# A two-layer diffusion trunk on one core: every SBUF pool laid out anew, with the moving operands and the next weights of TensorE at chosen distances modulo 256 bytes

## The chip, the core and the metric

The kernel runs on one core of one Trainium2 chip. The metric is the device time of one execution in microseconds; the time before is the median of three runs.

## The reference, cut to what matters

Two layers work on 512 latent tokens and 256 context tokens of width 1024, all in float32. Layer 0 is neighbourhood attention beside a spatial gating unit, layer 1 is a two-way retention over the latent tokens with a state carried in from the context; behind each comes a gated MLP with a depthwise convolution over the tokens. Every sub-layer stands between two RMS norms, and shift, scale and gate come from a conditioning vector.

```python
h = modulate(rmsnorm(x, norm_g[i, 0]), sh1, sc1)
y = hybrid_na_sgu(...) if i % 2 == 0 else retention_mixer(...)
x = x + g1 * rmsnorm(y, norm_g[i, 1])
h = modulate(rmsnorm(x, norm_g[i, 2]), sh2, sc2)
a = dwconv3(h @ ffn_w_in[i], conv_w, conv_b)        # 1024 -> 2 * 2816
gate, up = split(a)
x = x + g2 * rmsnorm((silu(gate) * up) @ ffn_w_out[i], norm_g[i, 3])
```

Nearly all of the arithmetic is in the products with the weight matrices.

## The kernel before, in words

**Products in three parts.** A float32 operand is split in two float32r tiles: `split` lets ScalarE (ACT) write the rounded value, hi, and VectorE (DVE) the rest, lo. `mm3` then issues three matmuls for every product: hi by hi, hi by lo, lo by hi. Its first argument is the stationary operand (128 columns, loaded by a weight load before each matmul), its second the moving one, of 256, 384 or 512 columns. The weight load of a matmul is issued while the matmul before it still streams. So while one matmul reads its moving operand, the weights of the next are read out of the same SBUF partitions.

**Weight units.** A unit is 128 x 1024 elements of a weight matrix. `raw_unit` loads it by a DMA of the SyncE (SP) queue into a `raw` tile, `unit` splits it into the hi and the lo tile of a slot. There are three slots in the lasting pool `bp` (tags `wh0`, `wl0` to `wh2`, `wl2`) and some more in a pool of the stage (`slot`, `phase`): two in the gating unit, three in the retention, and named rings in the MLPs (the inner function `slot` of `ffn`). In some products the unit is stationary and the activations move (the projections of attention, the queries and keys of the retention, the first products of the MLPs); in others the activations are stationary and the unit moves (gating unit, the retention's values and gates, all output projections).

**The stages in order.** Gating unit (output tiles `ug`, `mx`, `wsg`), attention (`pq`, `pk`, `pv`, for the context `px` and `py`; scores `s`, weighted values `o`, output `wat...`), MLP of layer 0 (`px`, `py`, `pz` of 384 columns, from a two-by-two block scheme with fewer multiplications; output `wf`), retention (values and gates `rn`, keys and queries `rk`, `rq`, context keys `rkc`, scores `rs`, states `stc`, `stl`, results `ro`, `rx`, output `wr`), MLP of layer 1 (`px`, `py`, `pz` of 256 columns, output `wf`). Vector products for shift, scale and gate run beside them as background jobs. Nearly every instruction is recorded under line 69, a helper, so the profile's groups are told apart by their tiles.

**Where tiles lie.** A pool takes its tags in the order of their first use, each with the room of all its buffers, and rounds a tile up to 32 bytes; pools follow one another, and a pool of a stage begins where the pools still open end. So every tile's byte address in its partition can be worked out from the sizes. Three lines of `retention` and three of `ffn` already create tiles early to fix an order. Below, the position of a tile is its address modulo 256, and the distance of a matmul is the position at which the weights of the next matmul begin, minus the position at which its own moving operand begins, modulo 256.

Of the kernel before, what the change touches and what calls it, by code (L numbers as in the profile page):

```python
# [18 lines left out]
KD = 8  # L19
# [14 lines left out]
EARLY = 2  # L34
MLP_PIECES = (
# [41 lines left out]
class Trunk:  # L77
    def __init__(self, ctx, tc, a, out):
        self.ctx, self.tc, self.nc, self.a, self.out = ctx, tc, tc.nc, a, out
        nc = self.nc  # L80
        self.V, self.S, self.T = (Ordered(tc, e) for e in (nc.vector, nc.scalar, nc.tensor))
        self.G = nc.gpsimd
        pool = lambda name, **k: ctx.enter_context(tc.tile_pool(name=name, bufs=1, **k))
        self.cp = pool("cp")
        self.bp = pool("bp")
        self.pp = pool("pp", space=bass.MemoryType.PSUM)
        self.dp = pool("dp", space=bass.MemoryType.DRAM)
        self.flip = 0

# [29 lines left out]
    def slot(self, name):  # L119
        i = self.turn % (3 + self.extra)  # L120
        self.turn += 1
        pool = self.bp if i < 3 else self.xp
        return [pool.tile([P, 1024], F32R, name=f"{name}{x}", tag=f"w{x}{i}", bufs=1) for x in "hl"]

    def phase(self, ctx, name, extra):
        self.xp = ctx.enter_context(self.tc.tile_pool(name=name, bufs=1))
        self.extra = extra
        self.turn = 0
        return self.xp

# [8 lines left out]
    def setup(self):  # L139
# [4 lines left out]
        c4 = self.cp.tile([P, KD, 4], F32R, name="c4", tag="c4")  # L144
        for s in range(2):
            S.activation(c4[:, :, 2 * s], cs[:, 8 * s : 8 * s + 8], AF.Copy)
            V.tensor_tensor(
                out=c4[:, :, 2 * s + 1],
                in0=cs[:, 8 * s : 8 * s + 8],
                in1=c4[:, :, 2 * s].bitcast(F32),  # L150
                op=ALU.subtract,
            )
        self.c4 = c4
        self.ident = self.const("ident", [P, P], a["ident"])
        self.adab = self.const("adab", [P, 16], a["adab_col"])
        self.ng = self.const("ng", [P, 64], a["ng_col"])
# [18 lines left out]
    def ada_first(self, q, pool, native, tag):  # L175
# [5 lines left out]
        for n in range(2):  # L181
# [24 lines left out]
            if not native:  # L206
                mt = self.bp.tile([P, 2, 4], F32, name=f"mt{n}{q}", tag="mt", bufs=2)
                S.copy(mt, pt)
# [31 lines left out]
    def ada_half(self, l, half, streams, gate=None, away=False, fine=False, side=False):  # L240
# [60 lines left out]
        gi = (l * 4 + (0 if m < 2 else 2)) * 8 + h * 4  # L301
# [227 lines left out]
    def block_sums(self, l):  # L529
# [30 lines left out]
        hb = self.bp.tile([P, 6144], F32R, name=f"hs{l}", tag="h1", bufs=1)  # L560
        for i, x in enumerate((2, 4)):
            self.blk["t", x] = hb[:, 8 * n * i : 8 * n * (i + 1)].rearrange("p (x k c) -> p x k c", x=2, k=4)
        self.rest = hb[:, 16 * n :]
# [142 lines left out]
    def sgu(self, y, xn):  # L706
        S, V, T, G, a = self.S, self.V, self.T, self.G, self.a
        toks = (4, 5, 0, 1, 2, 3)
        with ExitStack() as ctx:
            wp = self.phase(ctx, "sguw", 2)  # L710
            bcol = wp.tile([P, 8], F32, name="sgub", tag="sgub")
            self.load(bcol, a["sgu_b"])

            def ug_units(which, js):
                return [
                    self.unit(a["hyb_ug"][(which * 4 + i) * P : (which * 4 + i + 1) * P], f"ug{which}{i}") for i in js
                ]
# [9 lines left out]
            with ExitStack() as c2:  # L727
                fp = c2.enter_context(self.tc.tile_pool(name="firstp", bufs=1))
                self.alloc_h("a")
# [27 lines left out]
            sp = ctx.enter_context(self.tc.tile_pool(name="sgup", bufs=1))  # L757
            u = [sp.tile([P, 6, 256], F32, name=f"un{i}", tag=f"un{i}") for i in range(2)]
# [3 lines left out]
            for t in toks:  # L762
                ug(ps[t], t, w, (6, 7))
                gg = self.t2k(f"gg{t}")
                S.activation(gg, ps[t], AF.Gelu_apprx_tanh)
                bs = sp.tile([P, 6], F32, name=f"bs{t}", tag="bs", bufs=2)
                mv = sp.tile([P, 2], F32, name=f"mv{t}", tag="mv", bufs=2)
# [46 lines left out]
            wo = [self.unit(a["hyb_out"][(4 + f) * P : (5 + f) * P], f"wos{f}") for f in range(4)]  # L814
# [8 lines left out]
    def attention(self, y, final):  # L823
        a = self.a
        with ExitStack() as ctx:
            ap = self.ap = self.phase(ctx, "attp", 0)
            self.mask = ap.tile([P, 3, 256], F32, name="mask", tag="mask")
# [15 lines left out]
            for i in range(n + lag):  # L843
                if i < n:
# [3 lines left out]
                    if step == 0:  # L848
                        pr["at"] = [ap.tile([P, 768], F32R, name=f"at{x}{j}", tag=f"at{x}", bufs=4) for x in range(2)]
                        if j == 3:  # L850
                            A = (
                                [pairs[0]["at"], pairs[1]["at"]],
                                [self.unit(a["hyb_out"][f * P : (f + 1) * P], f"woa{f}") for f in (0, 1)],
                            )
                            fills = self.out_pieces(*A, y, toks[:1], False, None, "ata", "A")
# [220 lines left out]
    def retention(self, y, final):  # L1076
        S, V, T, G, a = self.S, self.V, self.T, self.G, self.a
        KS = float(np.float32(P) ** np.float32(-0.5))
        with ExitStack() as ctx:
            rp = self.phase(ctx, "retp", 3)  # L1080
# [10 lines left out]
            order = [("rv0", 1536), ("rv1", 1536), ("rg", 1024)] + [(f"w{x}{i}", 1024) for i in (3, 4, 5) for x in "hl"]  # L1091
            order += [("e0", ND), ("e1", ND), ("rk0", 512), ("rk1", 512), ("rq0", 512), ("rq1", 512), ("kd0", 1024), ("kd1", 1024)]
            for tag, w in order:
                rp.tile([P, w], F32, name=f"at{tag}", tag=tag, bufs=1)
# [3 lines left out]
                self.unit(a["ret_vg"][(o + h * 2 + i) * P : (o + h * 2 + i + 1) * P], f"rw{n}{h}{i}", dst)  # L1098
# [299 lines left out]
    def ffn(self, l, y, final, gates=None):  # L1398
# [13 lines left out]
        with ExitStack() as ctx:  # L1412
            fp = self.phase(ctx, f"ffnp{l}", 0)
            cw = fp.tile([P, 44, 4], F32, name=f"cw{l}", tag="cw")
            if not first:
                for tag in ("rawu", "wh5", "wl5", "wh6", "wl6", "pre0", "pre1"):
                    fp.tile([P, 1024], F32R if tag[0] == "w" else F32, name=f"at{tag}", tag=tag, bufs=1)
# [5 lines left out]
            if first:  # L1423
                G.memset(pres[0][:, :, 256:258], 0.0)
            else:
                for tag in ("cv", "wh4", "wl4"):
                    fp.tile([P, 1024], F32R if tag[0] == "w" else F32, name=f"at{tag}", tag=tag, bufs=1)
# [7 lines left out]
            def slot(kind, name):  # L1435
# [6 lines left out]
                if h[0] == "w":  # L1442
                    pool = self.bp if i < 3 else fp
                    return [pool.tile([P, 1024], F32R, name=f"{name}{x}", tag=f"w{x}{i}", bufs=1) for x in "hl"]
# [43 lines left out]
            def conv(j, pre):  # L1488
# [16 lines left out]
                else:  # L1505
                    g = [fp.tile([P, W], F32R, name=f"g{l}{i}{j}", tag=f"g{i}", bufs=ng) for i in range(2)]
# [103 lines left out]
            def w_out(f, kind="o"):  # L1610
                u = slot(kind, f"fo{l}{f}")
# [148 lines left out]
    def build(self):  # L1760
# [11 lines left out]
        def ahead(key, src, home):  # L1772

            dst = [self.bp.tile([P, 1024], F32R, name=f"{key}{x}", tag=f"w{x}{home}", bufs=1) for x in "hl"]
# [12 lines left out]
        with ExitStack() as ctx:  # L1787
# [18 lines left out]
            self.early = hook(("rwv00", ("ret_vg", 0), 0), ("rwv01", ("ret_vg", 1), 1))  # L1806
            self.between = lambda: ahead("rwk0", ("ret_qk", 8), 2)
# [74 lines left out]
def layout(i):  # L1882
# [8 lines left out]
    o["ng_col"] = cols(g["norm_g"])  # L1891
# [40 lines left out]
```

## Time and profile before

| what | value |
|---|---|
| median of three runs | 1865.7 us (1861.69 to 1869.01) |
| span of the profiled execution | 1867.9 us |
| TensorE matmuls | 1797.4 us busy, 96% of the span, 10928 instructions |
| TensorE weight loads | 1591.9 us busy, 85% |
| VectorE, ScalarE, GpSimd | 75%, 55%, 17% |
| mean granted clock of TensorE | 0.986 |

The profile gives no time for the profiled execution beside its span; the span stands 2.2 us above the median of the runs, inside their range. Matmuls are pipelined: the duration in a row runs from a matmul's start to its modelled end and is longer than the time until the next one starts. Rows of one tile give the smallest, the median and the largest duration. Two rows of one shape can be compared by their durations, and the true pace comes from the starts of successive groups in the timeline.

### The profile page before, as it was taken

Reading aid. Unit: us, or ns where it says so; the run is one execution under the profiler, and the core shown is the slowest. Engines: PE = TensorE matmul, PEld = TensorE weight load, DVE = VectorE, ACT = ScalarE, POOL = GpSimd, SP = SyncE. Lnnn points to the kernel's source line nnn. Section 1 sums busy time; section 2 is a strip of 40 time slices with the busy share of each in tenths; the row PEclk is TensorE's granted clock in tenths of the full one; section 3 lists DMA queues with packets and bytes.
Section 4 is the critical chain, followed back from the end, with each engine's and each line's share of the span. In section 5 each row is a group of like instructions: output and inputs, shape, how many; then the busy total and the mean of one; then the engine's idle time right before and its main releaser. Section 6 shows DMA issues by size and latency. Waiting matters only on the chain. (4 is left out here: it accounts for less than half of the span.)

```text
span 1867.9 us, 28825 instructions
## 1 busy us (share of the span) xinstructions
PE 1797.4 (96%) x10928; PEld 1591.9 (85%) x10928; DVE 1400.7 (75%) x2359; ACT 1031.0 (55%) x1866; POOL 325.9 (17%) x462
## 2 busy tenths in 40 slices
PE   7999999999999999999898999999999989999997
PEld 4887777689998899998788989988999879889996
DVE  4877775789868778777766676676655699988887
ACT  6533555677555565554564535344344477667763
POOL 1102222031122222221111011011001100222221
PEclk9999999999999999999899999999999989999999
DMA  8345321255677777786622423332321325978772
GB/s 293 113 139 149 108 85 40 69 157 154 170 148 194 167 164 159 156 169 149 243 98 76 156 79 99 116 95 70 113 69 46 102 81 153 224 192 197 172 162 97
DMA packets 84399, 253.47 MB, mean 136 GB/s; under 512 B 11026, under 2 KB 11538, under 8 KB 84260
## 3 DMA queue, kind: packets, MB, share of 16 engines
q1 hardware_dynamic: 55044, 191.29, 32.7%
q0 software_dynamic: 26912, 51.95, 16.4%
q10 hardware_dynamic: 2304, 8.39, 1.1%
q8 instruction: 86, 1.41, 0.3%
q14 instruction: 53, 0.43, 0.1%
HBM read 191.81 MB, written 39.85 MB: 124 GB/s over the span
## 5 line engine op out<-in xcount | busy, mean ns | idle before, releaser
L69 DVE SCALAR_TENSOR_TENSOR acc<-ar,cs,acc 128x512 f32<-128x512 f32 x256 | 185.5, 750 | 32.0 <-DMA ar<-in_adaw 17.4
L69 DVE SCALAR_TENSOR_TENSOR cv<-pre,cw,cv 128x769 f32<-128x769 f32 (+1 forms) x176 | 153.4, 881 | 9.9 <-ACT cv L69 9.2
L1645 POOL DMA_DIRECT2D yf<-yp x64 | 55.1, 861 | 257.0 <-ACT yp L69 235.5
L69 ACT ACTIVATE cv<-pre,cw 128x770 f32<-128x770 f32 (+1 forms) x88 | 81.2, 924 | 20.3 <-DVE pre L69 19.7
L69 ACT COPY yp<-wf 128x512 f32<-128x512 f32 x118 | 67.8, 577 | 23.7 <-PE wf L69 23.4
L69 ACT ACTIVATE pre<-px 128x256 f32<-128x256 f32 (+2 forms) x160 | 54.3, 366 | 48.1 <-PE px L69 47.4
L1645 POOL DMA_DIRECT2D yd<-yp x48 | 43.0, 902 | 132.1 <-ACT yp L69 129.1
L1645 POOL DMA_DIRECT2D yd<-ypg x48 | 41.9, 882 | 132.8 <-ACT ypg L69 124.3
L1265 POOL TENSOR_SCALAR rrr<-rmv 128x2 f32<-128x2 f32 x16 | 3.8, 237 | 274.1 <-DVE rmv L69 274.0
L69 ACT ACTIVATE g<-cv 128x770 fp32r<-128x770 f32 (+1 forms) x44 | 32.4, 736 | 29.1 <-DVE cv L69 29.1
L69 PE MATMUL px<-hs,wd 128*128 128x384 f32 x240 | 46.1, 340 | 0.2 <-DVE pre L69 0.2
L246 POOL MEMSET acc<- 128x512 f32 x32 | 19.3, 606 | 147.7 <-DVE al L69 128.9
L69 PEld LDWEIGHTS px<-hs,wd 128*128 128x128 f32 x240 | 43.0, 191 | 2.2 <-DVE pre L69 0.6
L69 DVE TENSOR_TENSOR pre<-pre,pz 128x256 f32<-128x256 f32 (+1 forms) x60 | 20.8, 372 | 29.9 <-PE pz L69 29.9
L69 DVE TENSOR_TENSOR g<-cv,g 128x770 fp32r<-128x770 f32 (+1 forms) x44 | 36.2, 822 | 8.3 <-ACT g L69 8.2
L69 ACT ACTIVATE pre<-py 128x384 f32<-128x384 f32 (+1 forms) x40 | 17.5, 437 | 43.4 <-PE py L69 23.1
L69 ACT ACTIVATE cv<-cv 128x770 f32<-128x770 f32 (+1 forms) x44 | 32.7, 743 | 14.2 <-DVE cv L69 14.1
L69 DVE TENSOR_TENSOR rv<-rn,rv 128x512 fp32r<-128x512 f32 x24 | 16.5, 687 | 30.2 <-ACT rv L69 30.2
L69 ACT ACTIVATE sc<-sc,sst 128x512 f32<-128x512 f32 x32 | 23.1, 723 | 27.7 <-DVE sc L69 27.7
L69 DVE TENSOR_TENSOR cv<-cv 128x770 f32<-128x770 f32 (+1 forms) x44 | 36.2, 823 | 1.1
L69 ACT COPY ypg<-wf 128x512 f32<-128x512 f32 x54 | 30.9, 577 | 9.7 <-PE wf L69 8.8
L69 ACT ACTIVATE rv<-rn 128x512 fp32r<-128x512 f32 x24 | 14.3, 594 | 38.5 <-PE rn L69 37.6
(2645 smaller groups left out, 6905.8 us busy)
## 6 DMA issues: line engine op xcount, KB each, us to landing
ar<-in_adaw SPq DMA_DIRECT2D x96, 512.0 KB, 3.8
yf<-yp POOLq DMA_DIRECT2D x64, 256.0 KB, 4.7
yd<-yp POOLq DMA_DIRECT2D x54, 256.0 KB, 5.2
yd<-ypg POOLq DMA_DIRECT2D x54, 256.0 KB, 4.9
fin<-xd SPq DMA_DIRECT2D x8, 512.0 KB
xn<-in_x SPq DMA_DIRECT2D x6, 512.0 KB, 4.6
xb<-in_x SPq DMA_DIRECT2D x6, 512.0 KB
xd<-xb ACTq DMA_DIRECT2D x6, 512.0 KB, 3.2
```

Of the source, the lines that this page charges most:

```text
L69: i = f(*args, **kw)
L246: G.memset(t, 0.0)
L1265: G.tensor_scalar(out=rr[:, 0, t2], in0=mv[:, t2, 1], scalar1=1.0, scalar2=EPS, op0=ALU.mult, op1=ALU.add)
L1645: G.dma_start((yd[t] if first else y[t])[:, o], v, accum_op=ALU.add)
```

## The change

**One slot, one tile.** hi and lo of a unit are no longer two tiles of 1024 elements but two parts of one tile (`place`): in the slots of `bp` and of the retention it has 2112 elements, and the unit begins `at` elements into it, 0, `Q1` = 16 or `Q3` = 48 (0, 64 or 192 bytes); the other slots have 2048 elements, and the pool's order sets their position.

**Every pool gets a written order.** A new helper `lay` creates one tile of each tag before all use, with nameless gaps of 16, 24, 40 or 48 elements, in `bp` and in the pools of the gating unit, the attention, the retention and both MLPs. No instruction is issued for these tiles.

**Small moves.** `c4` (the split conditioning vector) and `mt` go to the pool of the first stage, with the four instructions that fill `c4`; `bs` and `mv` of the gating unit go to `bp`; `ng` holds only the 32 of its 64 columns that are read; the second half of `h1` behind the blocks begins 64 bytes later; `g` of the first MLP lies 62 elements into a tile of 832, so that the latent tokens' columns begin at position 0 and the context's at 248.

The positions, worked out from the sizes (w0 to w2 are slots in `bp`):

| matmuls (columns) | stationary / moving | distance before | distance after |
|---|---|---|---|
| `rn` (256) | h / unit | 192 (w0, w1), 128 (w2), 224 (w3 to w5) | 64 |
| `ug` of the second half (256) | h / unit | 192, 128, 96 | 64 |
| `ug` of the first half, `wsg` (512) | h or sT / unit | 192, 128, 96 or 96, 32, 0 | 0 |
| `pq`, `pk` / `pv` (512) | unit / h | 64 / 128 | 0 |
| `px`, `py` of the attention (256) | unit / h | 64 and 128 | 0 |
| `s` (256) | q / k | 0 | 64 |
| `px`, `py`, `pz` of layer 0 (384) | unit / blocks | 0, 64, 128 | 64 (`wd` 0) |
| `px`, `py`, `pz` of layer 1 (256) | unit / blocks | 0 or 64 | 64 |
| `wf` of layer 0 (512) | g / unit | many | 0 (latent), 248 (context) |
| `wf` of layer 1 (512) | g / unit | 0 (w5, w6), 192 (w2) | 0 |
| `rk`, `rq` (512) | unit / h | 64, 128, 32 | 0 |
| `rkc` (256) | unit / h | 64, 128, 32 | 0 |
| `rs` (256) | k / q | 0 | 64 |
| `stc`, `stl`, `ro` (256) | kd, sd / v | 64 | 64 |
| `rx` (512) | q / st | 0 | 0 |
| `wr` (512) | gt / unit | 224 (w0, w1), 160 (w2), 0 (w3 to w5) | 0 |

The diff, cut to its core:

```diff
+SLOT = 2112
+Q1, Q3 = 16, 48
 ...
+        order = [("G0", 1024), ("h0", 6144), ("t2k", 512, 4), ("y0", 1024), ("y1", 1024), ("y2", 1024), ("y3", 1024)]
+        order += [("raw", 1024, 3), ("w0", SLOT), ("w1", SLOT), ("w2", SLOT), ("acc0", 512), ("h1", 6144 + Q1)]
+        order += [("ss", 2, 8), ("rsw", 1, 4), ("rsr", 1, 6), ("bs", 6, 2), ("mv", 2, 2)]
+        self.lay(self.bp, order)
...
-    def unit(self, src, name, dst=None):
+    def unit(self, src, name, dst=None, at=0):
         raw = self.raw_unit(src, name)
-        hi, lo = dst or self.slot(name)
+        hi, lo = dst or self.slot(name, at)
         self.split(hi, lo, raw)
...
+    def place(self, i, name, at=0):
+        pool, wide = (self.bp, SLOT) if i < 3 else (self.xp, self.wide)
+        if wide == 2048:
+            at = 0
+        t = pool.tile([P, wide], F32R, name=name, tag=f"w{i}", bufs=1)
+        return [t[:, at + 1024 * x : at + 1024 * x + 1024] for x in range(2)]
...
+    def lay(self, pool, order):
+        for n, (tag, width, *bufs) in enumerate(order):
+            if tag is None:
+                tag = f"gap{n}"
+            pool.tile([P, width], F32, name=f"at{tag}", tag=tag, bufs=bufs[0] if bufs else 1)
...
-        return [pool.tile([P, 1024], F32R, name=f"{name}{x}", tag=f"w{x}{i}", bufs=1) for x in "hl"]
+        return self.place(i, name, at)
...
+            order = [("dist", ND), ("cos", 512), ("sin", 512), ("dec", 16), ("gng", 16), (None, 24)]
+            order += [("rv0", 1536), ("rv1", 1536), ("rg", 1024), ("w3", SLOT), ("w4", SLOT), ("w5", SLOT)]
+            order += [("e0", ND), ("e1", ND), (None, 16), ("rk0", 512), ("rk1", 512), (None, 48), ("rq0", 512), ("rq1", 512)]
+            order += [("kd0", 1024), ("kd1", 1024), ("kc", 256), ("sd0", 512, 2), ("sd1", 512, 2), (None, 48), ("of", 1024)]
...
+                order = [("rawu", 1024), ("w5", 2048), ("w6", 2048), ("pre0", 1024), ("pre1", 1024), ("blk", 4096), ("cv", 1024)]
+                order += [(None, 16), ("w3", 2048), (None, 48), ("g0", W, 4), ("g1", W, 4), (None, 16), ("w4", 2048)]
+                order += [("cw", 176), ("yp", 2048)]
```

More of the change, by code (lines that the diff above doesn't have):

```diff
@@ L715, in ug_units @@
                 return [
-                    self.unit(a["hyb_ug"][(which * 4 + i) * P : (which * 4 + i + 1) * P], f"ug{which}{i}") for i in js
+                    self.unit(
+                        a["hyb_ug"][(which * 4 + i) * P : (which * 4 + i + 1) * P], f"ug{which}{i}", at=0 if which else Q3
+                    )
+                    for i in js
                 ]
@@ L1442, in slot @@
                 if h[0] == "w":
-                    pool = self.bp if i < 3 else fp
-                    return [pool.tile([P, 1024], F32R, name=f"{name}{x}", tag=f"w{x}{i}", bufs=1) for x in "hl"]
+                    return self.place(i, name, at)
                 pool = self.bp if i < 4 else self.lp
```

89 lines of the change are left out of this document (47 added, 42 removed).

## The prediction

> **What bounds the kernel now.** I read the page first, then the busy times by stage, then the timeline of one place, then the rows of single tiles.
>
> ```profile
> span 1867.9 us, 28825 instructions
> PE 1797.4 (96%) x10928; PEld 1591.9 (85%) x10928; DVE 1400.7 (75%) x2359; ACT 1031.0 (55%) x1866; POOL 325.9 (17%) x462
> PEclk9999999999999999999899999999999989999999
> PE 36%; DVE 5%; ACT 3%; DMA 2%; issue 1%; POOL 1%; DVEq 0%; ACTq 0%; POOLq 0%; SPq 0%
> ```
>
> TensorE is busy for 96% of the span at a granted clock that is full in nearly every slice, and it leads the chain of waits. By stage (first MLP's main loop, seven heads of the retention, second MLP's main loop; columns: stretch, its length, busy time and count of each engine, clock, DMA):
>
> ```profile
> 436.00:930.00 494.00, 478.82 (x2432) 438.70 (x2431) 397.62 (x567) 283.09 (x490) 110.39 (x146) 0.98 0.73 171
> 1030.00:1460.00 430.00, 428.59 (x2993) 393.99 (x2992) 269.42 (x460) 184.42 (x264) 39.98 (x56) 1.00 0.30 93
> 1545.00:1834.00 289.00, 285.88 (x2007) 264.34 (x2006) 255.51 (x400) 201.64 (x357) 57.31 (x68) 1.00 0.72 176
> ```
>
> PE runs for 478.82 of 494, 428.59 of 430 and 285.88 of 289 us; the next engine, DVE, has 20%, 37% and 12% to spare. So the time is the sum of the intervals at which matmuls follow each other, and a nanosecond off each of 10928 is 10.9 us.
>
> **Does that interval depend on where the operands lie?** In the timeline (start, length, engine, tile, count) two groups of the same twelve matmuls, at the same distance of 64, both before and after:
>
> ```profile
> 1208.76 1.52 PE L69 MATMUL ro<-rv,sd 128*128 128x256 f32 x12
> 1210.12 1.08 PE L69 MATMUL rx<-st,rq 128*128 128x512 f32 x4
> ...
> 1214.24 1.58 PE L69 MATMUL ro<-rv,sd 128*128 128x256 f32 x12
> 1215.66 1.55 PE L69 MATMUL rx<-st,rq 128*128 128x512 f32 x6
> ```
>
> From start to start it is (1210.12 - 1208.76) / 12 = 113 ns and (1215.66 - 1214.24) / 12 = 118 ns. So a distance does not fix the interval alone; a stream can run in one of two paces. Durations follow the interval: 113 ns goes with 276 and 118 with 281, 162 or 163 ns more each time, so rows can be compared by their medians. Now equal work in slots at different positions. The output projection of the retention (distance 0 in the first row, 224 in the second) and its context keys (64 and 128):
>
> ```profile
> L69 PE MATMUL wr<-rwo10h,gt x16: 388/389/497, 1097.6 to 1108.9; 128*128 128x512 f32 x16
> L69 PE MATMUL wr<-rwo20h,gt x16: 392/396/495, 1163.4 to 1175.0; 128*128 128x512 f32 x16
> ...
> L69 PE MATMUL rkc<-h0c,rwk1h x8: 276/276/383, 1011.3 to 1014.8; 128*128 128x256 f32 x8
> L69 PE MATMUL rkc<-h0c,rwk2h x8: 279/282/285, 1079.7 to 1082.2; 128*128 128x256 f32 x8
> ```
>
> At 512 columns 0 gives 389 and 224 gives 396; at 256 columns 64 gives 276 and 128 gives 282. In the second MLP (distance 0 for the first row, 64 for the others):
>
> ```profile
> L69 PE MATMUL px<-hs x228: 274/283/384, 1548.9 to 1825.8; 128*128 128x256 f32 x114
> L69 PE MATMUL px<-blk,wb4h x8: 280/282/287, 1569.8 to 1571.0; 128*128 128x256 f32 x8
> L69 PE MATMUL pz<-hb,wa4h x8: 276/276/276, 1567.1 to 1568.2; 128*128 128x256 f32 x8
> L69 PE MATMUL pz<-hb,wa5h x8: 281/281/281, 1582.4 to 1583.6; 128*128 128x256 f32 x8
> ...
> L69 PE MATMUL wf<-fo12h,g x16: 389/393/397, 1572.6 to 1600.4; 128*128 128x512 f32 x16
> L69 PE MATMUL wf<-fo13h,g x16: 387/389/397, 1573.3 to 1601.1; 128*128 128x512 f32 x16
> L69 PE MATMUL wf<-fo14h,g x16: 392/396/400, 1604.1 to 1631.8; 128*128 128x512 f32 x16
> L69 PE MATMUL wf<-fo15h,g x16: 388/397/401, 1604.8 to 1632.5; 128*128 128x512 f32 x16
> ...
> L69 PE MATMUL px<-hs,wc3h x8: 334/335/335, 461.4 to 463.1; 128*128 128x384 f32 x8
> L69 PE MATMUL py<-blk,wc3h x8: 334/334/334, 469.1 to 470.8; 128*128 128x384 f32 x8
> L69 PE MATMUL pz<-hb,wa3h x8: 336/337/343, 463.5 to 465.3; 128*128 128x384 f32 x8
> ```
>
> (The second row, `blk` with `wb4`, is at 0 as the first; `pz` at 64 holds 276 for wa4 and 281 for wa5, the two paces again.) Of the groups of six `wf`, fo12 and fo13 lie in w5 and w6, distance 0: the first three matmuls show 393, the last three 389; fo14 lies in w2, and the group shows 396 and 397. The last three rows are the first MLP, 384 columns: 335 at 64, 334 at 0, 337 at 128.
>
> **The price list**, in ns of duration. 256 columns: 64 costs 276 in one pace and 281 in the other, and I take 277, nearer to the common one; 0 costs 282 to 283, 128 costs 282, 224 and 192 cost 280. 512 columns: 0 costs 389 in a running stream and 391 in a group of six; every other distance 394 to 397. 384 columns: 334, 335, 337.
>
> **The change part by part.** Counts of the tiles, one row each: `rn` in the retention, `px` and `py` in the second MLP, `wr`, `wf` in the first and in the second MLP; then two rows of `rn` and `pq`, `rk` at their present distances (192, 64, 64), and `rs` at 0.
>
> ```profile
> 930.00:1545.00 615.00, 234.83 (x1920) 0.98 0.30 93
> 1545.00:1868.00 323.00, 120.08 (x912) 0.99 0.68 171
> 1545.00:1868.00 323.00, 59.84 (x456) 0.99 0.68 171
> 930.00:1545.00 615.00, 70.52 (x288) 0.98 0.30 93
> 394.00:930.00 536.00, 164.45 (x648) 0.98 0.72 171
> 1545.00:1868.00 323.00, 110.89 (x425) 0.99 0.68 171
> ...
> L69 PE MATMUL rn<-rwv20h,h0c x24: 279/280/365, 1110.4 to 1126.4; 128*128 128x256 f32 x24
> L69 PE MATMUL pq<-h0a,wq0h x8: 394/394/400, 159.5 to 165.2; 128*128 128x512 f32 x8
> L69 PE MATMUL rk<-h0c,rwk1h x8: 388/396/398, 1011.6 to 1019.5; 128*128 128x512 f32 x8
> L69 PE MATMUL rs<-rq,rk x96: 274/282/364, 993.9 to 1446.1; 128*128 128x256 f32 x96
> ```
>
> 1. `rn`, 1920 matmuls from 280 to 277: -5.8 us.
> 2. Second MLP: a quarter of `px` (`hs`, 228), another quarter (`blk` with `wb`, 228) and half of `py` (228) go from 0 to 64, 282.5 to 277: 684 x 5.5 = -3.8 us. The rest is at 64 already.
> 3. `wf`: in the second MLP six of nine groups (283 of 425 matmuls) have a unit in w2; 395 to 391 is -1.1 us. In the first MLP the latent tokens' two thirds (432 of 648), 395 to 391: -1.7 us. The context's 216 go to 248, which no row shows: 389 and 397 bound it, -1.3 to +0.4 us, and I take 0, as the nearest row, 396 at 224, is no better than now. Sum -2.8 us.
> 4. Other matmuls of 512 columns: `wr`, the four heads' groups with a unit outside w3 to w5 (192 of 288), -5 each: -1.0. `rk` and `rq`, 2 x 7 x 24, 395 to 390: -1.7. `pq`, `pk`, `pv`, 3 x 4 x 24, 394 to 390: -1.2. Gating unit and attention output, about 430, of which I give two thirds -3.5: -1.0. Sum -4.9 us.
> 5. Other matmuls of 256 columns: `rs` 96 x 5 and `s` 160 x 5 by the row of `rs`, second half of `ug` 288 x 3 by the row of `rn`: -2.1 us.
> 6. The wrong way, to distance 0: `rkc`, 7 x 24, of which 72 from 276 to 282 and 96 from 281 to 282, +0.5 us; the attention's context projections, 288, by the same rows, +1.1 us.
> 7. 384 columns: `px` and `pz` with `wa` (480) 337 to 335, -1.0; some 960 others 334 to 335, +1.0. Sum 0, bounds -2 and +2 us.
>
> Sum: -5.8 - 3.8 - 2.8 - 4.9 - 2.1 + 1.6 = -17.8 us.
>
> 8. The merged tile. ACT may now write a unit's hi only when the last reader of the old lo, one matmul later than the old hi's, is done: 0.1 to 0.2 us later on an engine that is idle for 45% of the span; nothing. If a first matmul of a unit had to wait for the lo write too, the cost is the 1.22 us of the first row here at each place where PE waits for the hi write already (six places, the two longest shown), so at most 6 x 1.22 = 7.3 us. I take 0, since it reads hi alone and each half keeps its own writer.
>
> ```profile
> L69 DVE TENSOR_TENSOR rwk5l<-rwk5r,rwk5h x1: 1222/1222/1222, 1243.1 to 1243.1; 128x1024 fp32r<-128x1024 f32 x1
> ...
> PE px L69 <- ACT wc2h L69: 2.2, 1, 2.2
> PE rkc L69 <- ACT rwk1h L69: 1.8, 1, 1.8
> ```
>
> 9. The new orders issue nothing. The four `c4` instructions keep their place on ACT and DVE, as nothing of these engines stood between. `cw` of the first MLP moves to room that the attention's `at` tiles hold until about 392 us; its load left SP's queue at 409.6 us, so nothing behind it there is held back:
>
> ```profile
> L91 SPq DMA_DIRECT2D cw<-in_conv_col x2: 328/328/328, 409.6 to 1510.1; - x2
> ```
>
> 10. What comes next: with PE faster by 1%, DVE is late more often in the second MLP, where it has 12% to spare. I give 1 us of the 4.9 gained there back, at most all of it.
>
> So -17 us: 1867.9 - 17 = 1851 for a span, which stood 2.2 us above the median, hence 1849 us.
>
> **A rule of the skill against this.** The rows above show the interval going with the slot. The Trainium skill ("TensorE: Matmul & The Clock Gate", section "Step-by-step: what each phase is for") says that PE has two independent read ports on SBUF and that loading the next weights takes no read bandwidth from the running matmul; by that rule distances cost nothing and the sum would be 0. The two `wr` heads, 389 against 396 for the same work, disagree with it.
>
> **The rivals.**
> - *No change.* The pace belongs to how a stream starts, not to the distance: the two `ro` groups differ by 5 ns at one distance, as much as the distances do. Then streams fall into either pace as often as now: 1866 us. Against it: `px<-hs` stays at a median of 283 over 228 matmuls, and the rows of `rkc` and `wr` go by slot. The Trainium skill's rule above gives the same time. Chance 0.09.
> - *Half of it.* The new 64-streams sit in the slow pace half of the time (278.5 instead of 277: the 4400 of parts 1, 2 and 5 and those at 64 already, x 1.5 = +6.6 us), or DVE takes back the second MLP's gain (+4): 1849 + 8 = 1857 us. The two rows of `pz` speak for some of it. Chance 0.10.
> - *Slower.* The merged tile makes PE wait for the DVE half of a unit. It decides where more than 22 of the 191 splits of a unit do so (22 x 1.22 = 27 us: 17 of gain and 9.3 beyond); at 22, 1876 us. Against it: PE waits for a hi write in six places, so the other units are ready early. Chance 0.07.
>
> **How the numbers follow.** My case, 0.74: -8 to -27 us. The lower end has all 256-column streams at 276 and 512 at 389 (4400 x 1 + 2200 x 1.5 = 8 more, and 1.3 of the context's `wf`), the upper one loses 4 in the second MLP, 4 to the slow pace and 2 at 384 columns: 1839 to 1858. To leave no more than 2 in 10 outside I go from 1837 to 1863, which holds the half gain and part of no change. A measurement can tell 0.5%, 9.3 us, so faster means under 1856.4: my case but for its upper edge and some of the half case, 0.77; same 0.16; slower 0.07.
>
> **What would show it.** Right: `px<-hs` in the second MLP at 276 to 278 instead of 283; `wr`, `rk`, `rq`, `pq` near 389 in every slot; `rn` near 277; `rkc` at 282 in every head; DVE's and ACT's rows unchanged. Wrong: `rn` still at 280 or more, or `rn` at 281 in most heads (the slow pace); a wait of PE on lo halves that stands among its longest.

## The result and the profile after

| | kernel before | changed kernel |
|---|---|---|
| median, first comparison (6 runs each) | 1864.68 us | 1852.68 us (1847.79 to 1857.28) |
| ratio, 95% interval | | 0.9936 [0.9919, 0.9952] |
| the same comparison again (19 and 12 runs) | 1869.65 us | 1860.30 us (1854.9 to 1867.1) |
| ratio, 95% interval | | 0.9958 [0.9942, 0.9975] |
| span of the profiled execution | 1867.9 us | 1845.9 us |

The change takes 9 to 12 us off, where 17 were forecast; both medians and both ratios say so. The two spans differ by 22 us, and that must not be read as the gain. The page and the mean granted clock of the changed kernel:

```profile
span 1845.9 us, 28788 instructions
PE 1777.3 (96%) x10928; PEld 1579.5 (86%) x10928; DVE 1398.2 (76%) x2359; ACT 1030.1 (56%) x1866; POOL 331.1 (18%) x462
PE 35%; DVE 7%; DMA 3%; ACT 2%; issue 1%; POOL 1%; DVEq 0%; POOLq 0%; ACTq 0%
core 0: 1845.9 us, clock 0.992
```

and of the kernel before:

```profile
core 0: 1867.9 us, clock 0.986
```

In both traces TensorE's granted clock falls to half in stretches of 3.4 or 6.8 us, ten of them before and four after (and one of 9 us at the very end of each). Each of the ten and the four begins within 7 us after a pause of TensorE of 1.4 us or more began, and pauses of 2 to 3 us are followed by one in some executions and by none in others, so their number differs from one execution to the next. 0.006 of 1850 us is 11 us, half of the 22. So below I compare matmul by matmul outside these stretches, and for whole kernels I give, beside the ratio, the mean over the runs of time times granted clock, which takes the half-clock stretches out: its standard error is 0.4 to 0.7 us. In the second comparison it is 1846.0 us before and 1838.5 us after, 7.5 us less.

The main loops of the first MLP, seven heads of the retention and the second MLP in the changed kernel (stretch, length, busy time and count of PE, PEld, DVE, ACT, POOL, clock, DMA):

```profile
436.00:919.00 483.00, 472.29 (x2453) 433.35 (x2452) 399.59 (x570) 284.70 (x497) 111.45 (x148) 1.00 0.72 175
1020.00:1445.00 425.00, 423.04 (x2999) 390.84 (x2998) 267.16 (x461) 179.63 (x259) 39.17 (x55) 1.00 0.28 94
1530.00:1814.00 284.00, 282.92 (x1998) 263.57 (x1998) 252.91 (x395) 199.38 (x353) 57.30 (x68) 1.00 0.71 177
```

PE is still busy for all but 11, 2 and 1 us of them. Now the rows that the prediction named as its tests (smallest, median, largest duration):

```profile
L71 PE MATMUL rn<-rwv,h0c x768: 276/276/580, 932.3 to 1426.0; 128*128 128x256 f32 x192
L71 PE MATMUL rn<-rwg,h0c x512: 276/281/367, 961.5 to 1440.8; 128*128 128x256 f32 x171
L71 PE MATMUL px<-hs x240: 276/281/384, 1529.6 to 1814.0; 128*128 128x256 f32 x120
L71 PE MATMUL wr<-rwo,gt x288: 387/389/502, 1014.0 to 1355.0; 128*128 128x512 f32 x144
L71 PE MATMUL rq<-h0c,rwq x112: 388/389/476, 1008.5 to 1407.8; 128*128 128x512 f32 x112
L71 PE MATMUL rkc<-h0c,rwk x128: 276/283/388, 938.7 to 1393.2; 128*128 128x256 f32 x128
```

512 columns (`wr`, `rq`) came to 389 as forecast, and `rkc` went the wrong way to 283, where 282 was forecast. At 256 columns the values of the retention (`rwv`) reach 276, its gates (`rwg`) 281, and the second MLP's `px<-hs` went from 283 to 281 instead of 277.

Busy time of PE with the tiles of one name, for `rn` over the whole retention and `px`, `py`, `pz` over the whole second MLP, in this order, before:

```profile
915.00:1560.00 645.00, 234.83 (x1920) 230.33 (x1920) 16.50 (x24) 23.84 (x40) 0.98 0.31 98
1505.00:1868.00 363.00, 128.14 (x960) 124.27 (x960) 8.28 (x20) 22.55 (x60) 0.99 0.64 162
1505.00:1868.00 363.00, 64.37 (x480) 60.17 (x480) 8.28 (x20) 7.67 (x20) 0.99 0.64 162
1505.00:1868.00 363.00, 31.35 (x240) 29.30 (x240) 8.33 (x20) 0.99 0.64 162
```

and after:

```profile
915.00:1560.00 645.00, 230.48 (x1920) 226.11 (x1920) 16.49 (x24) 23.84 (x40) 0.99 0.29 97
1505.00:1868.00 363.00, 127.31 (x960) 123.69 (x960) 8.28 (x20) 22.49 (x60) 0.98 0.60 156
1505.00:1868.00 363.00, 64.93 (x480) 60.51 (x480) 8.28 (x20) 7.62 (x20) 0.98 0.60 156
1505.00:1868.00 363.00, 32.00 (x240) 29.85 (x240) 8.33 (x20) 0.98 0.60 156
```

`rn` gained 4.3 us, half-clock stretches included. The second MLP's three together lost 0.4 us, from 223.86 to 224.24.

**The ledger.** From the start of one matmul to the start of the next, outside half-clock stretches and without intervals that hold a wait (over 133, 200 and 267 ns at 256, 384 and 512 columns), meaned over a group and multiplied by its count:

| group, step of the prediction | matmuls | ns before | ns after | us | forecast, us |
|---|---|---|---|---|---|
| `rn` (1) | 1920 | 117.3 | 115.4 | -3.6 | -5.8 |
| second MLP: `px` / `py` / `pz` / `pf` (2) | 960 / 480 / 240 / 192 | 117.3 / 117.0 / 114.3 / 116.0 | 117.2 / 117.2 / 117.0 / 117.8 | +1.0 | -3.8 |
| `wf`, first / second MLP (3) | 792 / 527 | 232.5 / 231.6 | 231.0 / 231.1 | -1.5 | -2.8 |
| `rk`, `rq` (4) | 336 | 232.7, 233.2 | 228.2, 227.6 | -1.7 | -1.7 |
| `pq`, `pk`, `pv` (4) | 288 | 233.3, 233.1, 232.2 | 229.1, 228.4, 228.2 | -1.2 | -1.2 |
| `wr` (4) | 384 | 231.7 | 228.5 | -1.3 | -1.0 |
| `ug` first half, `wsg`, `wat` (4) | 432 | 232 | 229 | -1.3 | -1.0 |
| `rs`, `s`, `ug` second half (5) | 544 | 118.1 | 117.0 | -0.6 | -2.1 |
| `rkc`, the attention's `px`, `py` (6) | 480 | 116.4 | 119.5 | +1.5 | +1.6 |
| 384 columns (7) | 1896 | 174.8 | 174.7 | -0.2 | 0 |
| all, with the small groups | | | | -9.0 | -17.8 |

So 9.0 us of pace were gained, beside 7.5 us of time times clock (error 0.6), and most of the missing half is at 256 columns.

### The profile page after: what moved, and what is told of

Its sections match the earlier page's. It is cut to its first block, busy times and chain, and to the rows that moved or that the text cites. A ratio compares the mean times of both kernels' runs of the same rounds, so it can differ in the third digit from the quotient of the medians.

```text
span 1845.9 us, 28788 instructions
## 1 busy us (share of the span) xinstructions
PE 1777.3 (96%) x10928; PEld 1579.5 (86%) x10928; DVE 1398.2 (76%) x2359; ACT 1030.1 (56%) x1866; POOL 331.1 (18%) x462
## 5 line engine op out<-in xcount | busy, mean ns | idle before, releaser
L71 PE MATMUL rn<-rwv,h0c 128*128 128x256 f32 x768 | 136.2, 281 | 2.9 <-ACT h0c L71 2.9
L71 PEld LDWEIGHTS rn<-rwv,h0c 128*128 128x128 f32 x768 | 118.1, 191 | 3.6 <-ACT h0c L71 3.3
L71 PE MATMUL wf<-fo,g 128*128 128x512 f32 x432 | 112.4, 394 | 0.1
L71 PE MATMUL rn<-rwv,h1c 128*128 128x256 f32 x384 | 108.1, 282 | 0.4 <-DVE h1c L71 0.2
L1680 POOL DMA_DIRECT2D yf<-yp x64 | 55.1, 861 | 254.4 <-ACT yp L71 231.1
L71 PE MATMUL rn<-rwg,h0c 128*128 128x256 f32 x512 | 89.8, 279 | 0.0
L71 PE MATMUL px<-hs,wc 128*128 128x384 f32 (+1 forms) x480 | 78.4, 311 | 5.1 <-ACT pre L71 2.7
L71 PEld LDWEIGHTS rn<-rwg,h0c 128*128 128x128 f32 x512 | 78.0, 189 | 0.0
L71 PE MATMUL pz<-hb,wa 128*128 128x384 f32 (+1 forms) x480 | 77.4, 308 | 0.0
L71 PE MATMUL px<-hb,wa 128*128 128x384 f32 (+1 forms) x480 | 77.2, 308 | 0.0
L71 PE MATMUL py<-blk,wb 128*128 128x384 f32 (+1 forms) x480 | 76.9, 308 | 0.0
```

Source lines behind the costliest of these rows:

```text
L71: i = f(*args, **kw)
L1680: G.dma_start((yd[t] if first else y[t])[:, o], v, accum_op=ALU.add)
```

## The experiments

### The merged tile alone

```diff
-        return [pool.tile([P, 1024], F32R, name=f"{name}{x}", tag=f"w{x}{i}", bufs=1) for x in "hl"]
+        t = pool.tile([P, 2048], F32R, name=name, tag=f"w{i}", bufs=1)
+        return [t[:, 1024 * x : 1024 * x + 1024] for x in range(2)]
```

in the kernel before (and the same in its three other places).

> The kernel before with one part of the change alone: hi and lo of a unit in one tile, at the addresses that they have anyway, so distances stay as they are. If the merged tile is free (step 8 of the prediction): 1865 us as before, within 3, waits of PE on splits as in the kernel before (2.2 and 1.8 us the longest). If PE waits for the lo half too (rival Slower): longer by 1.2 us at each unit that does so, 1870 us or more, with DVE halves among the longest waits of PE. If the layout of tiles gives part of the gain by itself: under 1862 us.

1862.47 us, ratio 0.9985 [0.9967, 1.0003]; time times clock 0.8 us less than before (1843.7 against 1844.5). No group's spacing moved by more than a nanosecond that is made of more than a hundred matmuls. Waits of PE on units:

```profile
PE px L69 <- ACT wc L69: 2.2, 1, 2.2
PE rkc L69 <- ACT rwk L69: 1.8, 1, 1.8
```

These are the two waits of the kernel before, to the tenth. DVE halves of units stand among PE's waits too, but the same ones as in the kernel before: `fo09l` 1.9 us here and 3.2 there, `wp` 1.1 here and 1.0 there, none of the rest over 0.5. The merged tile costs nothing and gives nothing that these runs can tell.

### Positions or distances

```diff
-        order = [("G0", 1024), ("h0", 6144), ...
+        order = [(None, 16), ("G0", 1024), ("h0", 6144), ...
```

> The changed kernel with every tile of the core's memory behind the constants 64 bytes further, so that all distances stay and all positions move. If distances count: spacings by group as in the change within 0.5 ns (rn 115.4, px 117.6, wr 228.5, rk 228.2, wf 231.0). If positions count: groups change by 2 to 5 ns.

`rn`, then `px`, `py`, `pz` of the second MLP:

```profile
915.00:1560.00 645.00, 230.50 (x1920) 226.15 (x1920) 16.48 (x24) 23.82 (x40) 0.98 0.31 97
1505.00:1868.00 363.00, 128.31 (x960) 124.54 (x960) 8.21 (x20) 22.50 (x60) 0.98 0.62 158
1505.00:1868.00 363.00, 65.12 (x480) 60.73 (x480) 8.21 (x20) 7.61 (x20) 0.98 0.62 158
1505.00:1868.00 363.00, 31.95 (x240) 29.80 (x240) 8.29 (x20) 0.98 0.62 158
```

230.50 against 230.48 us for `rn`, and by starts `rn` 115.3, `px` 117.0, `wr` 228.6, `rk` 228.1, `wf` 231.0: the same paces with every tile 64 bytes further. A common shift by 64 bytes does nothing to them. (This is one execution, of 1862.85 us; it and the other kernels below that have no ratio are read for their paces alone.)

### What chooses between the two paces of distance 64

The five `rn` blocks of a head (48 matmuls each: three of values, two of gates) in the changed kernel, mean spacing from the thirteenth matmul on:

| head | values | gates |
|---|---|---|
| 1, 2, 3, 4, 7 | 113.3, 113.3, 113.3 | 117.8, 117.8 |
| 5, 6 | 117.8, 117.8, 117.8 | 113.3, 113.3 |

Nothing lies between. Head 0 is left out, as its blocks come in another order; two executions of the changed kernel give its first, second and fifth block different paces (117.5, 113.6, 113.3 and 113.8, 118.0, 117.8). The same in rows: PE's busy time with `rn` in head 1, two blocks of values, the third, the two of gates:

```profile
1027.50:1039.50 12.00, 11.14 (x96) 10.97 (x97) 0.68 (x1) 0.60 (x1) 1.00 0.75 253
1039.50:1046.00 6.50, 5.62 (x48) 5.54 (x48) 0.68 (x1) 1.18 (x2) 1.00 0.47 171
1048.40:1060.50 12.10, 11.47 (x96) 11.37 (x96) 0.00 (x0) 1.06 (x2) 1.00 0.19 59
```

The gates' 96 matmuls take 11.47 us, the values' 96 take 11.14, though 0.1 us of wait and entry are in them; and it is the gates' stretch that has the smaller DMA share (0.19 against 0.75 in the last column but one). So DMA traffic isn't what slows this stream. I took the pace for a thing of the entry and disturbed it, with one narrow matmul at the head of each of the two gate blocks of a head:

```diff
                     for kk in range(KD):
                         wk = w[kk // 4]
+                        if dst == "g" and i + kk == 0:
+                            T.matmul(ps[:, 0, 0:64], hc(0)[0], wk[0][:, 0, 0:64], start=True, stop=True)
                         self.mm3(
```

> The changed kernel, with one extra matmul of 64 columns at the head of each of the two rn blocks of the gate (wg) in every head, overwritten by the next one: 16 more matmuls, all positions and distances as in the change. Theory B (two paces at 64; the entry chooses, the stream keeps): the gate's blocks, which hold 117.8 in heads 1 to 4 and 7 and 113.3 to 113.7 in heads 5 and 6, change pace in many heads, and rn's first three blocks keep theirs in each head. Rival (the pace belongs to the operands of a block): each block keeps its pace.

| head | values | gates |
|---|---|---|
| 1, 2, 3, 4, 7 | 113.3, 113.3, 113.3 | 113.3, 117.8 |
| 5, 6 | 117.8, 117.8, 117.8 | 117.8, 113.3 |

In rows of head 1, from the start of the first to the start of the second of each pair, 30 matmuls: the first gate block in the changed kernel (3.53 us, 117.7 ns), then in this run the first (3.40 us, 113.3 ns) and the second (3.53 us, 117.7 ns):

```profile
1050.65 0.40 PE L71 MATMUL rn<-rwg,h0c 128*128 128x256 f32 x2
1054.18 0.40 PE L71 MATMUL rn<-rwg,h0c 128*128 128x256 f32 x2
...
1059.93 0.39 PE L71 MATMUL rn<-rwg,h0c 128*128 128x256 f32 x2
1063.33 0.39 PE L71 MATMUL rn<-rwg,h0c 128*128 128x256 f32 x2
...
1065.55 0.40 PE L71 MATMUL rn<-rwg,h0c 128*128 128x256 f32 x2
1069.08 0.40 PE L71 MATMUL rn<-rwg,h0c 128*128 128x256 f32 x2
```

Operands, positions and distances are those of the change; the first gate block turned over in seven heads, from slow to fast in five and from fast to slow in two, the values kept their pace. The second gate block, which in the change goes on in the first one's pace, now runs in the other one: each extra matmul turned the pace of what came behind it. A stream at distance 64 has two paces, its entry picks one, and it stays.

In the second MLP I had tried the entry earlier, by moving the output weights and `g` together:

```diff
-order = [("rawu", 1024), ("w5", 2048), ("w6", 2048), ("pre0", 1024), ...
-order += [(None, 16), ("w3", 2048), (None, 48), ("g0", W, 4), ("g1", W, 4), (None, 16), ("w4", 2048)]
+order = [("rawu", 1024), (None, 16), ("w5", 2048), ("w6", 2048), (None, 48), ("pre0", 1024), ...
+order += [(None, 16), ("w3", 2048), ("g0", W, 4), ("g1", W, 4), ("w4", 2048)]
...
-                u = slot(kind, f"fo{l}{f}", 0)
+                u = slot(kind, f"fo{l}{f}", 0 if first else Q1)
```

> The changed kernel; in the second MLP the output weights and the gate g both lie 64 bytes further, so that wf keeps distance 0 inside its groups, and only the step from a group to the next px goes from distance 64 to 0 (and px to wf from 0 to 64). Theory A (the distance inside a stream sets its pace): px, py and pz keep a spacing of 117.6 in the mean, the time stays at 1853 within 3 us. Theory B (distance 64 has two paces, 113.3 and 117.8; a stream takes one when it is entered and keeps it): the entry is new, so most px, py, pz streams change pace: were all at 113.3, 1640 x 4.3 = 7 us less, 1846 us; were the entry to lead to 117.8 again, the first intervals of a stream are others and the sum is the same as now.

1860.49 us, ratio 0.997 [0.9956, 0.9983]. The groups of `wf` turned from intervals like 233, 236, 229, 232, 231, 226 to 227 throughout, 1.9 us in all, and `px`, `py`, `pz` mostly still entered into 117.8; the exceptions stand for the most part behind a wait of PE (intervals like 222, 117, 117, 123, 118, 114, 113). So at distance 0 the entry counts for `wf`, for `px`, `py` and `pz` the run speaks neither way, and it shows something else: 1.9 us of pace were gained and the time got no better than the changed kernel's 0.9936 and 0.9958 (time times clock 5.4 us under before, where the change has 7.5).

### The distance swept

`rn` alone, a distance per head, in two kernels:

```diff
-                self.unit(..., f"rw{n}{h}{i}", dst, Q3)
+                self.unit(..., f"rw{n}{h}{i}", dst, (48, 60, 56, 52, 44, 40, 36, 32)[h])
```

> The changed kernel with rn's distance different in each head of the retention: head 0 at 64 as in the change, heads 1 to 7 at 16, 32, 48, 80, 96, 112, 128 bytes. Read is the mean spacing of rn's matmuls in each head. Theory A (64 is the good distance): 113 to 118 at 64, 118 to 120 at all others. Theory C (what counts is whether two reads meet in one stretch of 64 bytes): 48 and 80 in between, 16 and 112 as 0 and 128. If no distance does better than 115 in all five blocks of a head, the pace is not for the layout alone to set.

> The same for heads 1 to 7 at 144, 160, 176, 192, 208, 224, 240 bytes. Theory A: 192 and 224 at 117 as in the kernel before, the others between 117 and 120. Theory C: 176 and 208 as 192, 240 as 0 (119.8). Any distance whose five blocks all hold 113.3 would be a better choice than that of the change: 1920 x 2.1 = 4 us less if used for every head.

The second one has (48, 28, 24, 20, 16, 12, 8, 4). Two rows of it, head 1 (144) and head 2 (160), all five blocks:

```profile
1036.90:1070.50 33.60, 27.91 (x240) 27.56 (x240) 2.05 (x3) 2.97 (x5) 1.00 0.53 162
1102.30:1137.00 34.70, 29.35 (x240) 28.98 (x240) 2.05 (x3) 2.95 (x5) 1.00 0.47 152
```

1.44 us between two heads for 240 matmuls, 6 ns each, by 16 bytes. Mean spacing by distance (64: seven heads of the changed kernel; 0: `rkc` and the attention's `px`):

| distance | 0 | 16 | 32 | 48 | 64 | 80 | 96 | 112 |
|---|---|---|---|---|---|---|---|---|
| ns | 119.6 | 117.1 | 118.3 | 117.7 | 115.5 | 119.3 | 118.5 | 117.9 |
| distance | 128 | 144 | 160 | 176 | 192 | 208 | 224 | 240 |
| ns | 118.7 | 113.9 | 119.9 | 119.2 | 116.9 | 118.3 | 117.2 | 117.5 |

64 is not the best one: 144 holds the fast pace in all five blocks. Neither theory holds: 16 and 192 stand under 118, and 176 and 208 do not go with 192. But a head is only five entries, and several distances have two paces as 64 has: at 48 three blocks hold 116.6 and two 119.3, at 192 one holds 113.3 and four 117.8. The third sweep asked for its neighbours, and for other widths at 144 (`at` 36 for `rk`, `rq` and the first MLP):

> The same with more moved to 144 to see other widths: rk, rq (512 columns, distance 0 in the change) and the first MLP's px, py, pz, pf (384 columns, 64 in the change); and rn's heads 0 to 7 at 144, 136, 140, 148, 152, 132, 156, 248. If the distance sets the pace of 512 columns as the prediction's price list has it, rk and rq go from 228 back to about 233 and their 336 matmuls cost 1.7 us; if the gain of rk and rq came from another part of the change, they stay at 228. 384 columns: 174.6 now; no forecast but that 144 lies between 170 and 177. Of rn's neighbours of 144: if the fast pace belongs to a stretch around 144, 140 and 148 hold it too.

132, 136, 140, 148, 152, 156 and 248 bytes gave 119.4, 121.3, 121.9, 119.9, 120.0, 120.6 and 119.0: a step of 4 bytes beside 144 costs 6 to 8 ns (all seven lie off the grid of 16 bytes of the first two sweeps). `rk` and `rq` went back to 233.3 and 233.2; 384 columns stayed at 174.6, where the change has 174.7.

### 144 put to use

```diff
-                self.unit(..., f"rw{n}{h}{i}", dst, Q3)
+                self.unit(..., f"rw{n}{h}{i}", dst, 28)
```

beside the changed kernel as it is:

> The changed kernel as it is, beside the next three. All theories: 12 us under the kernel before (1852.7 against 1864.7), ratio 0.9936, within 0.002.

1860.30 us, ratio 0.9958 [0.9942, 0.9975], a little further from 0.9936 than the 0.002 allowed.

> The changed kernel with rn at a distance of 144 bytes in every head, which in one head held 113.9 in all five blocks, where 64 gave 113.3 to 117.8. Theory D (144 has one pace only, the fast one): all 40 blocks of rn at 113.3 to 114.4, mean 113.9 instead of 115.4, so 1920 x 1.5 = 2.9 us under the changed kernel. Theory B' (144 has two paces too, and head 1 met the fast one by its entry): some blocks at 117 or more, and gain between 0 and 2 us.

1857.12 us, ratio 0.9939 [0.9916, 0.9961]; time times clock 1835.8, the changed kernel's 1838.5, before 1846.0. Head 1 again, the same three stretches:

```profile
1037.00:1048.60 11.60, 11.14 (x96) 10.97 (x96) 0.68 (x1) 0.59 (x1) 1.00 0.76 237
1048.60:1056.00 7.40, 5.65 (x48) 5.57 (x48) 0.68 (x1) 1.16 (x2) 1.00 0.63 204
1057.80:1070.00 12.20, 11.10 (x96) 10.99 (x96) 0.00 (x0) 1.20 (x2) 1.00 0.22 79
```

The gates come to 11.10 from 11.47; from its thirteenth matmul on every block of heads 1 to 7 holds 113.3 to 113.7 (two blocks of head 0 stand at 114.8 and 116.4), and the mean over all is 114.0. Pace says -2.8 us, time times clock -2.7 with an error of 0.8: within that error a nanosecond of pace in the retention is a nanosecond of time. Then 144 for the second MLP as well, by the weights (`at` 36 in slots of 2112, moving operands left at 0; and `at` 28 in `ug`'s second half):

> The same, and also 1780 matmuls of 256 columns elsewhere at 144 instead of 64: three quarters of px, and py, pz, pf of the second MLP, and three quarters of the second half of ug. Theory D: they go from 117.6 to about 114, 1780 x 3.6 = 6.4 us, so 9 us under the changed kernel, 1843 us; streams of twelve settle within some intervals, which may cost 1 us of it. Theory B': they keep 116 to 118, and the time is that of the run with rn alone. If DVE, 84% busy in the second MLP, takes it back: spacing falls as said and the time doesn't.

1856.67 us, ratio 0.994 [0.9919, 0.9961], time times clock 1836.3. `px`, `py`, `pz` of the second MLP:

```profile
1505.00:1868.00 363.00, 129.06 (x960) 125.42 (x960) 8.22 (x20) 22.47 (x60) 0.98 0.62 156
1505.00:1868.00 363.00, 66.35 (x480) 62.07 (x480) 8.24 (x20) 7.65 (x20) 0.98 0.62 156
1505.00:1868.00 363.00, 32.66 (x240) 30.50 (x240) 8.31 (x20) 0.98 0.62 156
```

Slower, not faster: `py` and `pz` at 120.0 and 119.8. The second half of `ug`, where six matmuls at another distance interrupt each group of 24, stayed at 116.6 (116.8 in the change). In `rn` the weights begin at 0 and the moving operand at 112; here the weights at 144 and the moving operand at 0. The distance is the same, the weights' place within 64 bytes is not. So I gave the second MLP weights at 192 and moving operands at 48:

```diff
-hb = self.bp.tile([P, 6144 // (8 * n), 2, 4, n], F32R, name=f"hb{l}", tag="h0", bufs=1)
+hb = self.bp.tile([P, 6160], F32R, name=f"hb{l}", tag="h0", bufs=1)[:, 12 * l : 12 * l + 6144]
...
-            def slot(kind, name, at=Q1):
+            def slot(kind, name, at=16 if first else 48):
```

(`hs` and `blk` alike; `bs` and `mv` back in their old pool to make room.)

> rn at 144 as before it, and the second MLP's px, py, pz, pf at distance 144 with the weights on a boundary of 64 bytes: moving operands at 48, weights at 192 (in the run before, moving at 0 and weights at 144, spacing 119.9). The quarter of px that reads the units in the rest of hs gets distance 16. Theory E (the weights' start within 64 bytes counts, and then the distance): py, pz, pf and three quarters of px at 113.5 to 115, 1500 x 3 = 4.5 us under the run with rn alone, so 0.9915 of the kernel before. Theory F (rn's pair of positions is good for itself, the distance is no measure): they stay between 117 and 120, and the time is that of the run with rn alone, 0.994, or 1 to 3 us more.

```profile
1505.00:1868.00 363.00, 125.92 (x960) 122.42 (x960) 8.23 (x20) 22.44 (x60) 0.98 0.62 156
1505.00:1868.00 363.00, 63.43 (x480) 59.20 (x480) 8.24 (x20) 7.59 (x20) 0.98 0.62 156
1505.00:1868.00 363.00, 31.20 (x240) 29.12 (x240) 8.30 (x20) 0.98 0.62 156
```

`py` and `pz` at 113.5 and 113.7, `px` at 115.1 with its quarter at distance 16: the pace expected came out, 4.1 us under the run with `rn` alone for the stage (`wf` gave 0.3 of it back), and with the run before it shows that beside the distance the pair's place within 64 bytes counts. At one distance the two starts shift together, so these runs don't tell whether it is the weights' start or the moving operand's. The time: 1852.99 us, ratio 0.9933 [0.9912, 0.9954], time times clock 10.7 us under before, where the run with `rn` alone had 10.2. So of 3.8 us of pace half a microsecond is left, which is less than the two means can tell. From the stage's first `pf` to its last output groups it took 336.4 us, with `rn` alone 336.9, in the changed kernel run again 335.8, with the same loss to half clock (6.2 to 6.6 us): it did not get shorter. But single executions can't tell 3.8 us here: less the loss to half clock, the same stretch takes 329.1 to 333.6 us in the seven traces whose second MLP is that of the change, and 330.1 here. What carries the reading is the time times clock of the runs. The waits of ACT between 1630 and 1690 us, with `rn` alone:

```profile
ACT fo L71 <- DMA fo110r<-in_ffn_out: 4.0, 1, 4.0
```

and in this run, with the wait of PE that follows:

```profile
ACT fo L71 <- DMA fo110r<-in_ffn_out: 6.3, 1, 6.3
```

```profile
PE px L71 <- ACT pre L71: 2.0, 1, 2.0
```

and in the kernel before:

```profile
ACT fo110h L69 <- DMA fo110r<-in_ffn_out: 4.4, 1, 4.4
```

A weight unit's load lands late; ACT waits for it with the splits, and the copies that free PE's accumulators stand behind. This wait of ACT is in all fourteen traces: 2.0 to 4.7 us in twelve, the kernel before among them, and 5.9 and 6.3 us in the two whose second MLP runs faster than the change's, the one with the faster `wf` and this one. So I take it that the faster PE arrives earlier at the same load. What the intervals of PE over 300 ns have beyond 240 adds up, in the stage, to 11.7 us here, 8.9 with `rn` alone, 7.2 in the changed kernel; over the same twelve traces it lies between 6.7 and 11.1, and with the faster `wf` it is 11.9. That fits, but it is argued and not shown: no run loads this unit earlier. That the pace does not reach the time is shown by the two kernels at 144, where the stage's pace went up and down by 4 us and time times clock by half a microsecond each.

### All of it taken back by addresses

Merged tile, orders and layout as in the change, only offsets in slots put to slow ones (in the second MLP the slots are 2112 wide for that, and the gaps between the tiles go): `rn` and `ug` at 160, the second MLP's weights at 144, `rk`, `rq`, `pq`, `pk`, `pv`, `wr` at 64:

```diff
-    f"rw{n}{h}{i}", dst, Q3)
+    f"rw{n}{h}{i}", dst, 24)
...
-    f"rw{n}{h}")
+    f"rw{n}{h}", at=Q1)
...
-    f"rwo{h}{f}")
+    f"rwo{h}{f}", at=Q3)
```

> The changed kernel with its merged tiles and its layout, but with operands put back to slow positions by their offset in a slot alone: rn and the second half of ug at distance 160 (119.9 in one head before), second MLP's weights at 144 (119.9), rk, rq, pq, pk, pv, wr (512 columns) at 64 instead of 0 with the weights on a boundary of 64 bytes; rkc and the attention's context projections come to 64 with that. If addresses alone set these paces and PE's pace sets the time: rn +8.6 us (1920 x 4.5), second MLP +3.8, ug +0.5, the 512 columns +4.8 (950 x 5.1), the context's -1.5: 16 us over the changed kernel, ratio to the kernel before 1.003 to 1.006. If the time hangs on something else of the change (merged tile, less excess waits): it stays near 0.995 while the spacings rise.

1868.44 us, ratio 1.0006 [0.9994, 1.0018], where 1.003 to 1.006 was expected: the whole gain is gone, by addresses alone. `rn`:

```profile
915.00:1560.00 645.00, 239.11 (x1920) 234.59 (x1920) 16.49 (x24) 23.89 (x40) 0.98 0.30 95
```

Spacings rose as expected, each in its group: `rn` to 119.9 (+8.5 us), 512 columns to 233.0 to 233.5 (+5.1), second MLP +4.0, `ug` +0.7, the context's -1.5; 16.7 us in all. Time times clock rose by 3.3 us over before, that is by 10.8 over the changed kernel (error 1.0). The second MLP's 4.0 hardly count, as the two kernels above show; of the other 12.7 us some 2 are not in the time, twice the error, and where they went I did not find.

## Why the prediction was right, and where it was not

The result lies in the range and on the side forecast, 3.7 us above the number given; by its mechanism it is the rival "Half of it" (1857 us), whose streams at 64 sit in the slow pace half of the time. The pace gained is half of the 17.8 us of the sum, and the second comparison's ratio would make it 1857 us; that the first median came within 3.7 us is in part luck. Of the signs named, `wr`, `rq` and `rkc` came out, and `px<-hs` (281 for 276 to 278) and the gates of `rn` (281 for 277) did not.

- **What bounds the kernel** (PE's interval) was right for the retention, where pace and time moved one to one within the error, and not for the second MLP, where of 4 us of pace half a microsecond was left.
- **Step 4 and step 6** were right to a few tenths: 512 columns at distance 0 are worth 5 ns in running streams, and the context's projections lose what was said.
- **Step 8 and step 9** at nothing: right. The kernel before with the merged tile is 0.8 us faster by time times clock, 0.7 its error.
- **Step 1 failed by its price.** I took 277 for distance 64, "nearer to the common one". `rn` met the slow pace in two blocks of five, or three of five, 115.4 in the mean instead of 114.5. -3.6 for -5.8 us.
- **Step 2 failed by its model.** I priced a distance by itself. In the kernel before, streams at 0 and at 64 alternated, and those at 64, each newly entered, mostly ran at 113.3 (`pz` 114.3). With all at 64, 115 of 135 groups of `px`, `py` and `pz` ran in the slow pace (`pz` 117.0), so what those at 0 won, the rest lost: +1.0 for -3.8 us. That the repeating cycle of groups leads each into the slow pace is my reading; no run shows it. That streams "sit in the slow pace" was the rival's mechanism: it counted on half of them, with a chance of 0.10, and here it was six in seven.
- **Step 3** was half right: in the change a group of six at distance 0 pays its entry each time (231 in the mean, 228 in streams of 24), so 391 in a group was too good. -1.5 for -2.8 us. With the entry moved it paid nothing (227).
- **Step 5**: the same two paces, -0.6 for -2.1 us.
- **Step 10** was too small: not 1 us of a gain in the second MLP would be given back, but nearly all of it, and, as far as the traces tell, to a late load before ACT rather than to DVE. In the change itself it cost nothing, since nothing was gained there.
- **The rule of the Trainium skill** weighed there ("TensorE: Matmul & The Clock Gate", "Step-by-step: what each phase is for": two independent read ports, no bandwidth taken by the next weights), by which distances would cost nothing, is not what these runs show: one operand moved by 16 bytes turned 113.9 into 119.9 ns, and the addresses took the gain back whole.

## What to carry to other kernels

Where PE runs in unbroken streams of float32r matmuls with a new weight load each, the places of the two operands are worth up to 8% of the interval (113.3 to 121.9 ns at 256 columns), so sweep them on the chip, one distance per repeated block, and read the spacing of starts. Keep the weights on a boundary of 64 bytes; then, in these streams and among the distances tried, 0 is best at 512 columns and 144 at 256, if the stream is long enough to settle. Price a change of pace only where the stage's other engines and loads have room for it, and compare runs by time times clock when the loss to half clock is as large as the effect: by that the version with `rn` and the second MLP at 144 (ratio 0.9933) is the fastest here, ahead of the change by 3 us with an error of 1, nearly all from `rn`.

## What the runs showed of the hardware that I had not expected

- A matmul stream of 256 columns at distance 64 has two exact paces, 113.3 and 117.8 ns, holds one over 48 to 96 matmuls without change, and turned over, in seven heads of seven, when a single narrow matmul was put at its head. At 144 it fell into 113.3 within about a dozen matmuls in all 35 blocks of heads 1 to 7.
- 4 bytes beside 144 cost 6 to 8 ns, 16 bytes 5 to 6; and distance 144 with the weights at 144 runs at 119.9, with the weights at 0 or 192 at 113.5 to 114.0. 384 columns took no notice of that (174.7 at 64, 174.6 at 144).
- The mean paces of the groups in the ledger repeat in two executions of the changed kernel to half a nanosecond (`rn` 115.4 and 115.5, `wr` 228.5 twice); what differs more are the half-clock stretches and the waits. What in the memory or in TensorE's reads makes two paces, no run here shows.
